# A hybrid encoder layer in float32 on one core: gate and up of 16 of 22 F-tile pairs by seven block products in place of eight

## The chip, the cores and the metric

The kernel runs on one core of a Trainium2 chip. The metric is the time of one execution in microseconds (us) of device time. Five engines take part: TensorE (PE, with its weight loads shown apart as PEld), VectorE (DVE), ScalarE (ACT), GpSimd (POOL) and SyncE (SP), whose queue issues the transfers.

## The reference, cut to what matters

The layer is four sublayers one after the other, each with a norm ahead of it and one behind it: a SwiGLU FFN, a mixer (neighbourhood attention beside a mean pool), a second SwiGLU FFN, and a gated embedding. Tokens are 512, features 1024, and the FFN has 2816 hidden features. Everything is float32.

```
def rms_norm(x, g):
    xf = x.astype(jnp.float32)
    y = xf * lax.rsqrt(jnp.mean(xf * xf, axis=-1, keepdims=True) + RMS_EPS)
    return (y * g.astype(jnp.float32)).astype(x.dtype)

def swiglu(x, w_gate, w_up, w_down):
    return (jax.nn.silu(x @ w_gate) * (x @ w_up)) @ w_down

h = x + 0.5 * rms_norm(swiglu(rms_norm(x, g1pre), ...), g1post)
h = h + rms_norm(hybrid_mixer(rms_norm(h, gmpre), ...), gmpost)
h = h + 0.5 * rms_norm(swiglu(rms_norm(h, g2pre), ...), g2post)
h = h + rms_norm((p @ W_proj) * sigmoid(rms_norm(h, gppre) @ W_gate), gppost)
```

## The kernel before, in words

Everything is kept transposed: features on the 128 partitions, the 512 tokens along the free axis, so the residual h is eight tiles of 128x512. A float32 product is made of three TensorE matmuls on float32r operands: each operand is split into a high part (the value rounded) and a low part (what is left), and `mm3` (lines 227 to 231) multiplies high by high (L228), high weight by low input (L229) and low weight by high input (L230).

**The weight stream.** All weights of the layer are one list of chunks of 128x1024 float32 (512 KB). `Stream.load` (L182) has SP load a chunk into one of NRAW=2 raw tiles; `Stream.pump` splits it, the high part `whi` by a cast on ACT (L195), the low part `wlo` by a subtraction on DVE (recorded as L160, the helper `tt` of all two-input operations). There are NB=8 pairs of split tiles. A chunk holds the stationary tiles of two k tiles times four output tiles.

**The FFN** (`ffn`, L411). The 22 F tiles of gate and up go in 11 groups of two tile pairs. A group (`group`, L344, `emit_group`, L308) makes four output tiles (gate and up of two F tiles) in four PSUM banks from 4 chunks: 8 k tiles x 4 output tiles x 3 matmuls = 96 matmuls of 512 columns. The input of those matmuls is `uh`/`ul`, the split of h times the norm's gain, without the norm's factor of the token. That factor, `rb` (one value per token, on every partition), is multiplied onto gate by DVE (`t<-g,rb`); then ACT makes Silu (L422), DVE multiplies by up (`v<-g,t`), ACT casts to `zh` (L430) and DVE makes `zl`. The factor of the up half is put off to the norm behind the sublayer (`norm` with `scaled`, tile `veps`). After groups 0 to 2, 3 to 6 and 7 to 10 (`PARTS`) come the down products of that part, with `zh`/`zl` as input and `f` as the running sum, each in two halves of the output. The last down group of a sublayer (`last_group`, L369) runs by halves of the tokens, in matmuls of 256 columns, so that the norm and the residual update of the first half (`boundary`, L395) go beside the products of the second.

**What sets the order.** The kernel emits its work with a clock of its own (`Clock`, `Task`, the table `TIMES`), and a scheduler then fixes the order on each engine. Each engine works through its list in order, and so do the queues of SP and POOL. The splits run ahead of the products by as many chunks as there are split tiles. At a sublayer's end `last_group` holds its chunks to the end, and the splits that run ahead meanwhile (`ahead`, L387) are for the first products of the next sublayer; in the mixer the eight bias tiles `bm` are loaded early by 64 small loads on SP into tiles with the tag "y".

Of the kernel before, what the change touches and what calls it, by code (L numbers as in the profile page):

```python
# [27 lines left out]
NB = 8  # L28
NRAW = 2
SPLIT_AHEAD = 4  # L30
# Where steps go between the products: distances on the emission clock, by sublayer boundary, head pair or channel group.
# [14 lines left out]
    "out": 3.8,  # L46
    "held": 2,
# [6 lines left out]
class Task:  # L54
    """Work emitted in steps: a generator that yields how long (us of products) to wait before its next step."""
# [7 lines left out]
class Clock:  # L63
    """Orders the emission: time advances with the products emitted, and due steps of tasks go between them."""
# [50 lines left out]
def kernel(  # L115
# [50 lines left out]
    class Stream:  # L166
        def __init__(self):
            self.loaded = 0
            self.split = 0
            self.done = 0  # L170
            self.hold = False
            self.freed = set()
            self.raw = {}
            self.parts = {}

        def load(self, upto):
            while self.loaded < min(upto, n_chunks):
                c = self.loaded
                self.raw[c] = wraw.tile([P, CH], F32, tag="raw", name=f"raw{c}")
# [3 lines left out]
                self.loaded += 1  # L183

        def pump(self, upto):
            while self.split < min(upto, self.done + NB, n_chunks):
                c = self.split
                self.load(c + 1)
                raw = self.raw.pop(c)
# [3 lines left out]
                for i in range(0, CH, w):  # L193
                    sl = slice(i, i + w)
                    nc.scalar.copy(hi[:, sl], raw[:, sl])  # L195
                    tt(lo[:, sl], raw[:, sl], f32(hi[:, sl]), ALU.subtract)
                self.parts[c] = (hi, lo)
                self.split += 1
                self.load(self.split + NRAW)
# [54 lines left out]
    veps = act.tile([P, NT], F32, name="veps")  # L254
# [17 lines left out]
    def norm(sl, rc, wait, scaled=False):  # L272
# [11 lines left out]
        if scaled:  # L284
            for b in range(nb):
                nc.scalar.activation(sd[:, b:b + 1], ps[:, b:b + 1], AF.Sqrt, bias=veps[:, b0 + b:b0 + b + 1],
                                     scale=1.0 / D)
        else:
            nc.scalar.activation(sd[:, :nb], ps[:, :nb], AF.Sqrt, bias=eps, scale=1.0 / D)
        if rc is not None:  # L290
            nc.vector.tensor_scalar(veps[:, b0:b0 + nb], ps[:, :nb], EPS / D, EPS * EPS, op0=ALU.mult, op1=ALU.add)
# [16 lines left out]
    def emit_group(c0, nch, rhs, ps, sl, free, evac=None, before=None):  # L308
        """All output tiles together, k outermost; with evac, one output tile after the other."""
# [8 lines left out]
        if evac is None:  # L318
            for c in range(nch):
                for kk in range(2):  # L320
                    if before:
                        before(2 * c + kk)
                    for t in range(4):
                        one(c, kk, t)
                if free:
# [11 lines left out]
    def half_banks():  # L337
        """Four accumulators of 256 columns in two banks; the first product of a bank opens both."""
# [5 lines left out]
    def group(c0, nch, rhs, evac, late=()):  # L344
        ps = [bank("g") for _ in range(4)]
        emit_group(c0, nch, rhs, ps, slice(0, S), True)
# [5 lines left out]
    def first_group(c0, rhs, evac, chains):  # L352
        """The first products of a sublayer, by halves of the tokens, as its input comes."""
# [15 lines left out]
    def last_group(c0, nch, rhs, evac, chain):  # L369
        """The last products of a sublayer, by halves of the tokens; returns the tasks that follow each."""  # L370
# [16 lines left out]
    def ahead():  # L387
        """Splits of the chunks that the next sublayer begins with."""
        upto = min(ws.done + NB, n_chunks)
# [5 lines left out]
    def boundary(f, gpost, gnext, scaled):  # L395
        def chain(sl, i):
            yield from norm(sl, None, at("nb", i), scaled)
# [13 lines left out]
    def ffn(chains, gpost, gnext):  # L411
        f = [None] * KD
        late = ()
        for pi, (g0, g1) in enumerate(PARTS):
# [3 lines left out]
            def ev_gu(t, ps, sl, j0, held={}):  # L418
                if t % 2 == 0:
                    g = ttile("t")  # L420
                    tt(g[:, sl], ps, rb[:, sl], ALU.mult)
                    nc.scalar.activation(g[:, sl], g[:, sl], AF.Silu)  # L422
# [3 lines left out]
                if j not in zh:  # L426
                    zh[j], zl[j] = ztile(j)
                v = vtile("v")
                tt(v[:, sl], ps, g[:, sl], ALU.mult)
                nc.scalar.copy(zh[j][:, sl], v[:, sl])  # L430
                tt(zl[j][:, sl], v[:, sl], f32(zh[j][:, sl]), ALU.subtract)

            for gi in range(g0, g1):
                j0 = 2 * (gi - g0)

                def ev(t, ps, sl, j0=j0):
                    ev_gu(t, ps, sl, j0)

                c0 = take(4)
                if gi > 0:  # L440
                    group(c0, 4, u_rhs, ev, late if gi == 1 else ())
                elif len(chains) == 2:
                    late = first_group(c0, u_rhs, ev, chains)
                else:
# [3 lines left out]
                    for t in range(4):  # L448
                        ev(t, ps[t], slice(0, S))

# [10 lines left out]
            for og in range(2):  # L461
# [8 lines left out]
                if lastp and og == 1:  # L470
                    return last_group(take(nch), nch, z_rhs, ev, boundary(f, gpost, gnext, True))
                group(take(nch), nch, z_rhs, ev)

# [1 line left out]
    def mixer(chains, gpost, gnext):  # L475
# [10 lines left out]
        def pieces(t0, t1):  # L486
            """(query order, token order) slices of a [.., 4, 8, 16] view for tokens of tiles t0..t1."""
# [130 lines left out]
        def windows(g, ps):  # L618
            """Centred means of group g minus the tokens themselves, in token order, split."""
# [141 lines left out]
        def m_rhs(k):  # L761
# [4 lines left out]
                          boundary(f, gpost, gnext, False))  # L766

# [91 lines left out]
    chains = ffn([clk.spawn(start(), TIMES["start"])], lambda k: gh[:, k:k + 1], GMPRE)  # L859
    chains = mixer(chains, GMPOST, G2PRE)  # L860
    chains = ffn(chains, lambda k: gh[:, 8 + k:9 + k], GPPRE)
    ple(chains)
    assert cur[0] == n_chunks == ws.done, (cur[0], n_chunks, ws.done)


# [1 line left out]
def _tok(a):  # L867
    """(512, F) with rows in sequence order -> (F, 512), tokens in the order (tile of 16 columns, row, column)."""
# [9 lines left out]
def _stationary(w, cols, nt=4):  # L878
    """Tiles [k][128][cols] -> chunks (2 k tiles each) of [128][k][tile][128]."""
    k = w.shape[0] // P  # L880
    a = np.stack([w[:, c:c + P] for c in cols], 1).reshape(k // 2, 2, P, nt, P)
    return a.transpose(0, 2, 1, 3, 4).reshape(k // 2, P, CH)

# [101 lines left out]
```

## Time and profile before

| what | value |
|---|---|
| three runs | 1114.8, 1114.62, 1113.77 us; median 1114.62 us |
| profiled execution | span 1111.1 us from the first to the last instruction; no time of its own beside the span is given |
| mean granted clock of TensorE | 0.995 of 2.4 GHz |
| PE busy | 1094.0 us (98%), 5610 matmuls |
| DVE busy | 578.6 us (52%) |
| ACT busy | 454.1 us (41%) |
| POOL busy | 0.7 us |
| loaded from and written to memory | 104.93 MB and 2.10 MB, 96 GB/s over the span |

The span leaves out what lies before the first and behind the last instruction, so it stands 3.5 us below the median of the runs. A busy time is the sum of an engine's instruction times, and matmuls overlap: what a stage costs is read from the starts of its instructions. PEclk is the share of its full clock that TensorE was granted.

### The profile page before, as it was taken

The page shows a single profiled execution, that of the slowest core. Times are in us where ns is not written, and L with a number is a line of the kernel's source. Part 1 is how long each engine was busy: PE and PEld are TensorE (multiplying, and loading weights), DVE is VectorE, ACT ScalarE, POOL GpSimd, SP SyncE. Part 2 cuts the span into 40 slices and gives each one's busy share as a digit, 9 for nine tenths or more (in the row PEclk, how much of TensorE's full clock was granted, in tenths as well). Part 3 has the DMA queues.
Part 4 walks back from the last instruction along what each step waited for, and adds up shares of the span by engine and source line. Part 5 has one row for each costly group of instructions (what it writes and reads, how often), then busy time and mean ns, then how long its engine had stood idle before and what let it go on. Part 6 is the DMA issues. An engine that isn't in the chain of part 4 may idle for free.

```text
span 1111.1 us, 14120 instructions
## 1 busy us (share of the span) xinstructions
PE 1094.0 (98%) x5610; PEld 930.1 (84%) x5610; DVE 578.6 (52%) x1041; ACT 454.1 (41%) x765; POOL 0.7 (0%) x6
## 2 busy tenths in 40 slices
PE   9999999999999999999999999999999999999995
PEld 7888888888889988887888899888888888889994
DVE  6642334333434987977444439632334333434976
ACT  7533223212323665366232257523223212323784
POOL 0000000000000000000000000000000000000000
PEclk9999999999999999999999999999999999999998
DMA  6553222232332043231223210533232222332112
GB/s 221 184 162 118 95 95 95 95 94 95 97 97 73 20 133 114 76 95 59 95 95 95 95 58 31 176 117 96 95 95 95 94 95 95 97 99 72 38 58 76
DMA packets 37010, 107.94 MB, mean 97 GB/s; under 512 B 4816, under 2 KB 11472, under 8 KB 36944
## 3 DMA queue, kind: packets, MB, share of 16 engines
q1 hardware_dynamic: 36800, 107.01, 29.8%
q8 instruction: 44, 0.72, 0.3%
q14 instruction: 22, 0.18, 0.1%
q10 hardware_dynamic: 144, 0.03, 0.0%
HBM read 104.93 MB, written 2.10 MB: 96 GB/s over the span
## 4 chain that ended last, share of the span: by engine, by line
PE 94%; DVE 2%; ACT 2%; issue 1%; DMA 0%; SPq 0%; DVEq 0%; ACTq 0%
PE g L228 25%; PE g L230 25%; PE g L229 25%; PE gate L228 2%; PE gate L229 2%; PE gate L230 2%; PE br L228 1%; PE br L230 1%; PE br L229 1%; DVE o L160 1%; ACT e L567 1%; PE v L229 1%; PE xp L228 1%; PE v L228 1%; PE v L230 1%; PE xp L230 1%
## 5 line engine op out<-in xcount | busy, mean ns | idle before, releaser
L160 DVE TENSOR_TENSOR wlo<-raw,whi 128x1024 fp32r<-128x1024 f32 (+1 forms) x195 | 235.3, 1208 | 340.8 <-ACT whi L195 340.2
L195 ACT CAST whi<-raw 128x1024 fp32r<-128x1024 f32 (+1 forms) x195 | 202.1, 1038 | 422.6 <-PE g L229 301.1
L228 PE MATMUL g<-uh,whi 128*128 128x512 f32 (+1 forms) x960 | 345.9, 362 | 0.4 <-ACT whi L195 0.4
L229 PE MATMUL g<-ul,whi 128*128 128x512 f32 (+1 forms) x960 | 346.3, 361 | 0.0
L230 PE MATMUL g<-uh,wlo 128*128 128x512 f32 (+1 forms) x960 | 345.7, 361 | 0.5 <-DVE wlo L160 0.5
L230 PEld LDWEIGHTS g<-uh,wlo 128*128 128x128 f32 x960 | 180.7, 188 | 28.6 <-DVE wlo L160 0.9
L228 PEld LDWEIGHTS g<-uh,whi 128*128 128x128 f32 x960 | 180.7, 188 | 28.3 <-ACT whi L195 0.9
L229 PEld LDWEIGHTS g<-ul,whi 128*128 128x128 f32 x960 | 180.8, 188 | 27.5 <-DVE ul L163 0.2
L228 PE MATMUL g<-zh,whi 128*128 128x512 f32 (+1 forms) x512 | 179.9, 351 | 0.0
L230 PE MATMUL g<-zh,wlo 128*128 128x512 f32 (+1 forms) x512 | 179.0, 350 | 0.0
L229 PE MATMUL g<-zl,whi 128*128 128x512 f32 (+1 forms) x512 | 177.9, 347 | 0.0
L230 PEld LDWEIGHTS g<-zh,wlo 128*128 128x128 f32 x512 | 96.0, 188 | 14.1
L229 PEld LDWEIGHTS g<-zl,whi 128*128 128x128 f32 x512 | 96.1, 188 | 13.6
L228 PEld LDWEIGHTS g<-zh,whi 128*128 128x128 f32 x512 | 96.3, 188 | 12.1
L160 DVE TENSOR_TENSOR acc<-acc,sq 128x256 f32<-128x256 f32 (+1 forms) x96 | 44.7, 466 | 17.9 <-ACT sq L269 16.7
L422 ACT ACTIVATE t<-t 128x512 f32<-128x512 f32 (+1 forms) x46 | 27.9, 610 | 63.5 <-DVE t L160 63.4
L160 DVE TENSOR_TENSOR t<-g,rb 128x512 f32<-128x512 f32 (+1 forms) x46 | 30.5, 667 | 39.6 <-PE g L230 38.4
L228 PE MATMUL gate<-uh,whi 128*128 128x512 f32 x128 | 50.6, 395 | 0.0
L230 PE MATMUL gate<-uh,wlo 128*128 128x512 f32 x128 | 50.0, 390 | 0.0
L229 PE MATMUL gate<-ul,whi 128*128 128x512 f32 x128 | 49.9, 390 | 0.0
L430 ACT CAST zh<-v 128x512 fp32r<-128x512 f32 (+1 forms) x46 | 27.3, 596 | 27.9 <-DVE v L160 27.8
L160 DVE TENSOR_TENSOR zl<-v,zh 128x512 fp32r<-128x512 f32 (+1 forms) x46 | 30.5, 665 | 13.1 <-ACT zh L430 13.1
(150 smaller groups left out, 960.8 us busy)
## 6 DMA issues: line engine op xcount, KB each, us to landing
raw<-in_wst SPq DMA_DIRECT2D x191, 512.0 KB, 3.4
h<-in_x SPq DMA_DIRECT2D x8, 256.0 KB, 5.7
bm<-in_bias SPq DMA_DIRECT2D x64, 32.0 KB, 3.3
out<-o SPq DMA_DIRECT2D x16, 128.0 KB, 1.7
raw<-in_wst SPq DMA_DIRECT2D x4, 128.0 KB, 3.5
g_sb<-in_gains ACTq DMA_DIRECT2D x1, 34.0 KB, 3.0
edge_sb<-in_edge SPq DMA_DIRECT2D x1, 32.0 KB, 5.9
```

The lines of the kernel that those rows point to most:

```text
L160: nc.vector.tensor_tensor(o, a, b, op=op)
L195: nc.scalar.copy(hi[:, sl], raw[:, sl])
L228: nc.tensor.matmul(o, wh, xh, start=first, stop=False, **kw)
L229: nc.tensor.matmul(o, wh, xl, start=False, stop=False, **kw)
L230: nc.tensor.matmul(o, wl, xh, start=False, stop=last, **kw)
L422: nc.scalar.activation(g[:, sl], g[:, sl], AF.Silu)
L430: nc.scalar.copy(zh[j][:, sl], v[:, sl])
L567: nc.scalar.activation(e[:, ii, :], e[:, ii, :], AF.Exp, bias=mn[:, ii:ii + 1], scale=-1.0, accum_out=sm[:, ii:ii + 1])
```

## The change

Groups 3 to 10 of both FFNs (`FAST`), which is 8 of 11 groups each, are computed by `fast_group`. Such a group is a product of a 2x2 block matrix of weights (rows: the two F tiles, gate and up beside each other; inner: the two halves of the 1024 features) by a 2x2 block matrix of inputs (inner halves by the left and the right 256 tokens). Seven block products stand in for eight. Each block product is 2 output tiles (gate, up) x 4 k tiles x 3 = 24 matmuls of 256 columns, 168 in a group.

The rest of the change serves those groups:

- **Sums of weights.** A fast group needs its four weight blocks and four sums of blocks. Two sums (`s3`, `s1`) are made in the load: SP loads one block, and then an accumulating transfer on GpSimd's queue (L210) adds the other onto it. Two are made by DVE on raw tiles (`source`). A fast group so takes five plain loads on SP's queue and two accumulating ones on GpSimd's, seven splits (seven casts on ACT, seven subtractions on DVE) and two additions of 128x1024 on DVE, where a group before took four loads and four splits.
- **Sums of products.** The products gather in three PSUM banks p, q, r. ACT copies three intermediate results away (`kept`: m1, m16, m7), and the next products are added onto the same banks; DVE makes three of the four result blocks (`made`) and the fourth is p itself. Then come Silu and the product with up per block, 128x256 each.
- **Sums of inputs.** `normalized` makes the normed input `un` with the factor rb, `renew` splits it over again into `uh`/`ul` during group 1, and `combined` makes four sums of its blocks and splits them, in tiles with the tags "y", "pth", "ptl" and "e". From group 2 on the input has the factor rb in it, so gate needs no multiplication by rb, and groups 0 and 1 get one more; the norm behind the sublayer has no `scaled` any more.
- **Buffers.** NB falls from 8 to 6 split tiles, NRAW rises from 2 to 6 raw tiles, loaded two ahead.

The core of the diff:

```diff
+FAST = range(3, 11)
-NB = 8
-NRAW = 2
+NB = 6
+NRAW = 6
+RAW_AHEAD = 2
...
+        ITEMS = ((0, 2), (0, 1), (1,), (2,), (3,))
+        LOADS = (4, 5, 5, 5, 5, 5, 5)
...
-                    nc.sync.dma_start(self.raw[c][:, i:i + w], wst[c][:, i:i + w])
+                    nc.sync.dma_start(self.raw[n][:, i:i + w], wst[c][:, i:i + w])
+                for c in more:
+                    nc.gpsimd.dma_start(self.raw[n], wst[c], accum_op=ALU.add)
...
+            if i == 2:
+                tt(a11, a11, s1, ALU.add)
+            if i == 6:
+                tt(a12, a12, a11, ALU.add)
+            return ((a11, ()), (a12, ()), (a11, ()), (s3, (c,)), (s1, (c + 1,)), (a22, (c + 2,)),
+                    (a12, (c + 3, c + 4)))[i]
...
+        def product(i, o, first):
+            wh, wl = ws.get(c0 + i)
+            for t in range(2):
+                for kk in range(4):
+                    w = slice((kk * 2 + t) * P, (kk * 2 + t + 1) * P)
+                    xh, xl = moving(i, kk)
+                    mm3(o[:, t * 256:(t + 1) * 256], wh[:, w], wl[:, w], xh, xl,
+                        first and kk == 0 and t == 0, kk == 3, skip_group_check=True)
+            ws.free(c0 + i)
...
+        product(0, p, True)
+        m1 = kept("m1", p)
+        product(1, q, True)
+        made(0, 0, q, m1, ALU.add)
+        product(2, p, False)
+        m16 = kept("m16", p, acc)
+        product(3, r, True)
+        m7 = kept("m7", r)
+        product(4, p, False)
+        made(1, 1, m7, p, ALU.subtract)
+        product(5, r, False)
+        made(1, 0, r, m16, ALU.subtract)
+        product(6, p, False)
+        done(0, 1, p, True)
...
+        def renew(k):
+            for c in chains:
+                clk.need(c)
+            while k not in un:
+                clk.need(whole, whole.steps + 1)
+            nc.scalar.copy(uh[k], un[k])
+            tt(ul[k], un[k], f32(uh[k]), ALU.subtract)
```

**ACT in a gate and up group.** Before, ACT casts one chunk after another until the next group's Silu (`t<-t`) comes; this is a stretch in the middle part of the first FFN:

```order
L195 CAST whi_1756<-raw_1692 128x1024
L195 CAST whi_1786<-raw_1730 128x1024
L195 CAST whi_1816<-raw_1760 128x1024
L195 CAST whi_1868<-raw_1790 128x1024
L195 CAST whi_1898<-raw_1820 128x1024
L195 CAST whi_1928<-raw_1872 128x1024
L422 ACTIVATE t<-t 128x512
```

In the changed kernel the same engine, at the passage from one fast group to the next (`raw_1568` and `raw_1574` hold the next group's blocks a11 and a12, L473 are the copies m1, m16 and m7, L580 are Silus):

```order
L242 CAST whi_1503<-raw_1323 128x1024
L553 CAST zh<-v 128x512
L242 CAST whi_1537<-raw_1331 128x1024
L473 COPY m_1477<-p 128x512
L242 CAST whi_1570<-raw_1568 128x1024
L580 ACTIVATE w<-w 128x256
L242 CAST whi_1604<-raw_1574 128x1024
L473 COPY acc<-p 128x512
L242 CAST whi_1638<-raw_1568 128x1024
L473 COPY m_1578<-r 128x512
```

The copies of PSUM banks now stand behind casts of chunks that have just been loaded: the copy of m16 (`acc<-p`) comes after the casts of a11 and a12 of the next group.

**The queues of SP and POOL.** SP's loads of one fast group in the changed kernel, in order (a22, a11 and a12 of a group, then the first blocks of the sums s3 and s1 of the next):

```order
L208 DMA raw_1323<-in_wst 128x1024
L208 DMA raw_1325<-in_wst 128x1024
L208 DMA raw_1331<-in_wst 128x1024
L208 DMA raw_1333<-in_wst 128x1024
L208 DMA raw_1436<-in_wst 128x1024
```

and POOL's, where each row is the second block of a sum, added onto the tile that SP loaded:

```order
L210 DMA raw_1090<-in_wst 128x1024
L210 DMA raw_1193<-in_wst 128x1024
L210 DMA raw_1333<-in_wst 128x1024
L210 DMA raw_1436<-in_wst 128x1024
```

Before, POOL's list held no transfer. Now each accumulating one waits for the plain load of the same tile, and the cast of the sum waits for both.

**DVE at the end of the first FFN.** Before, from the last residual tile of the first half of the tokens to the first input tile of the second half:

```order
L163 SCALAR_TENSOR_TENSOR h_87<-t,gh,h_87 128x256
L294 RECIPROCAL rc<-sd 128x2
L160 TENSOR_TENSOR acc<-acc,sq 128x256
L163 SCALAR_TENSOR_TENSOR ul_102<-h_86,g_sb,uh_94 128x256
L163 SCALAR_TENSOR_TENSOR ul_103<-h_87,g_sb,uh_95 128x256
L163 SCALAR_TENSOR_TENSOR dl<-ident,rc,dh 128x128 x2
L160 TENSOR_TENSOR acc<-acc,sq 128x256
L160 TENSOR_TENSOR wlo_3039<-raw_2539,whi_3038 128x1024
L160 TENSOR_TENSOR t<-f_764,rb 128x256
```

and in the changed kernel:

```order
L167 SCALAR_TENSOR_TENSOR h_87<-t,gh,h_87 128x256
L330 RECIPROCAL rc<-sd 128x2
L164 TENSOR_TENSOR wlo_3733<-raw_3303,whi_3732 128x1024
L167 SCALAR_TENSOR_TENSOR ul_102<-h_86,g_sb,uh_94 128x256
L167 SCALAR_TENSOR_TENSOR dl<-ident,rc,dh 128x128 x2
L167 SCALAR_TENSOR_TENSOR ul_103<-h_87,g_sb,uh_95 128x256
L164 TENSOR_TENSOR acc<-acc,sq 128x256
L164 TENSOR_TENSOR wlo_3790<-raw_3362,whi_3789 128x1024
L164 TENSOR_TENSOR t<-f_852,rb 128x256
```

Two splits of weights stand in this stretch instead of one.

## Rows read from the trace of the kernel before

**Rows 1.** The page: span, busy time of each engine, chain that ended last.

```profile
span 1111.1 us, 14120 instructions
...
PE 1094.0 (98%) x5610; PEld 930.1 (84%) x5610; DVE 578.6 (52%) x1041; ACT 454.1 (41%) x765; POOL 0.7 (0%) x6
...
PE 94%; DVE 2%; ACT 2%; issue 1%; DMA 0%; SPq 0%; DVEq 0%; ACTq 0%
```

**Rows 2.** Timeline of PE, groups 3 to 6 of the first FFN: start, duration.

```profile
105.64 0.40 PE L228 MATMUL g<-uh,whi 128*128 128x512 f32 x1
105.87 0.39 PE L229 MATMUL g<-ul,whi 128*128 128x512 f32 x1
...
192.73 0.40 PE L228 MATMUL g<-zh,whi 128*128 128x512 f32 x1
```

**Rows 3.** By stretch: length, busy (count) of PE, PEld, DVE, ACT, POOL, PEclk, DMA, GB/s.

```profile
28.45:72.44 43.99, 43.99 (x197) 36.42 (x196) 24.18 (x27) 20.19 (x24) 0.00 (x0) 1.00 0.59 187
105.64:192.50 86.86, 86.86 (x384) 71.89 (x383) 32.17 (x36) 24.87 (x31) 0.00 (x0) 1.00 0.30 97
```

**Rows 4.** Timeline of PE, last down group of the first FFN: 256 columns, first and last.

```profile
345.77 0.28 PE L228 MATMUL g<-zh,whi 128*128 128x256 f32 x1
345.89 0.28 PE L229 MATMUL g<-zl,whi 128*128 128x256 f32 x1
...
360.14 0.28 PE L230 MATMUL g<-zh,wlo 128*128 128x256 f32 x1
```

**Rows 5.** Timeline of PE, last group of the fourth sublayer: 256 columns of `uh`.

```profile
1071.44 0.28 PE L229 MATMUL g<-ul,whi 128*128 128x256 f32 x1
...
1087.04 0.28 PE L230 MATMUL g<-uh,wlo 128*128 128x256 f32 x1
```

**Rows 6.** Groups of DVE by form: busy, mean ns, idle before and what ended it.

```profile
L160 DVE TENSOR_TENSOR wlo<-raw,whi 128x1024 fp32r<-128x1024 f32 x191 | 233.7, 1224 | 340.7 <-ACT whi L195 340.2
L160 DVE TENSOR_TENSOR acc<-acc,sq 128x256 f32<-128x256 f32 x80 | 33.7, 421 | 13.5 <-ACT sq L269 12.6
L160 DVE TENSOR_TENSOR t<-g,rb 128x512 f32<-128x512 f32 x42 | 28.9, 691 | 39.5 <-PE g L230 38.4 <-ACT rb L305 1.1
L160 DVE TENSOR_TENSOR zl<-v,zh 128x512 fp32r<-128x512 f32 x42 | 28.9, 688 | 13.1 <-ACT zh L430 13.1
L163 DVE SCALAR_TENSOR_TENSOR ul<-h,g_sb,uh 128x512 fp32r<-128x512 f32 x8 | 5.8, 751 | 1.4 <-ACT uh L261 1.4
```

**Rows 7.** Groups of ACT by form.

```profile
L195 ACT CAST whi<-raw 128x1024 fp32r<-128x1024 f32 x191 | 200.5, 1051 | 422.5 <-PE g L229 301.1 <-PE gate L229 42.9 <-PE br L229 28.0
L430 ACT CAST zh<-v 128x512 fp32r<-128x512 f32 x42 | 25.8, 614 | 27.9 <-DVE v L160 27.8
L455 ACT COPY f<-g 128x512 f32<-128x512 f32 x16 | 9.4, 585 | 11.1 <-PE g L230 10.3
L793 ACT ACTIVATE g<-g 128x256 f32<-128x256 f32 x16 | 6.4, 411 | 4.2 <-DVE g L160 4.2
```

**Rows 8.** The page's DMA issues: KB each, median us to landing.

```profile
raw<-in_wst SPq DMA_DIRECT2D x191, 512.0 KB, 3.4
```

**Rows 9.** L182, all weight loads: duration of an issue in ns, and landing.

```profile
L182 SPq DMA_DIRECT2D raw<-in_wst x195: 327/328/432, 1.2 to 1062.9; - x195
...
DMA to landing us min/median/max: 2.8/3.4/6.1
```

**Rows 10.** Timeline of DVE at the end of the first FFN.

```profile
376.83 1.22 DVE L160 TENSOR_TENSOR wlo<-raw,whi 128x1024 fp32r<-128x1024 f32 x1
377.96 0.42 DVE L160 TENSOR_TENSOR t<-f,rb 128x256 f32<-128x256 f32 x1
...
379.70 0.48 DVE L163 SCALAR_TENSOR_TENSOR ul<-h,g_sb,uh 128x256 fp32r<-128x256 f32 x1
...
388.13 0.49 DVE L163 SCALAR_TENSOR_TENSOR ul<-h,g_sb,uh 128x256 fp32r<-128x256 f32 x1
```

**Rows 11.** Timeline of PE there: first uses of those two `ul` tiles.

```profile
381.45 0.28 PE L229 MATMUL g<-ul,whi 128*128 128x256 f32 x1
...
389.30 0.28 PE L229 MATMUL g<-ul,whi 128*128 128x256 f32 x1
```

More of the change, by code (lines that the diff above doesn't have):

```diff
@@ L172, in __init__ @@
             self.freed = set()
+            self.over = set()
             self.raw = {}
@@ L176, in load, with drop, source @@
         def load(self, upto):
-            while self.loaded < min(upto, n_chunks):
-                c = self.loaded
-                self.raw[c] = wraw.tile([P, CH], F32, tag="raw", name=f"raw{c}")
+            while (self.loaded < min(upto, len(self.items))
+                   and (self.loaded < NRAW or self.loaded - NRAW in self.over)):
+                n = self.loaded
+                c, *more = self.items[n]
+                self.raw[n] = wraw.tile([P, CH], F32, tag="raw", name=f"raw{n}")
                 w = CH // 4 if c < 1 else CH
                 for i in range(0, CH, w):
-                    nc.sync.dma_start(self.raw[c][:, i:i + w], wst[c][:, i:i + w])
+                    nc.sync.dma_start(self.raw[n][:, i:i + w], wst[c][:, i:i + w])
+                for c in more:
+                    nc.gpsimd.dma_start(self.raw[n], wst[c], accum_op=ALU.add)
                 self.loaded += 1
+        def drop(self, *items):
+            for n in items:
+                del self.raw[n]
+                self.over.add(n)
+        def source(self, n):
+            kind, c, i = self.ops[n]
+            if not kind:
+                return self.raw[c], (c,)
+            s3, s1, a22, a11, a12 = (self.raw.get(c + j) for j in range(5))
+            if i == 2:
[4 more added lines that the diff above has]
+                    (a12, (c + 3, c + 4)))[i]
         def pump(self, upto):
-            while self.split < min(upto, self.done + NB, n_chunks):
+            while self.split < min(upto, self.done + NB, self.n):
                 c = self.split
-                self.load(c + 1)
-                raw = self.raw.pop(c)
+                self.load(self.needs[c])
+                assert self.loaded >= self.needs[c]
+                raw, over = self.source(c)
                 hi = wsp.tile([P, CH], F32R, tag="whi", name=f"whi{c}")
@@ L196, in pump @@
                     tt(lo[:, sl], raw[:, sl], f32(hi[:, sl]), ALU.subtract)
+                self.drop(*over)
                 self.parts[c] = (hi, lo)
                 self.split += 1
-                self.load(self.split + NRAW)
+                self.load(self.needs[c] + RAW_AHEAD)
         def get(self, c):
@@ L283, in norm @@
         sd = tmp.tile([P, NT], F32, tag="sd", name="sd")
[L284 to L291, printed above, removed]
+        nc.scalar.activation(sd[:, :nb], ps[:, :nb], AF.Sqrt, bias=eps, scale=1.0 / D)
         if rc is None:
@@ L408, in boundary, with fast_group, kept, made @@
         return chain
-    def ffn(chains, gpost, gnext):
+    LEFT, RIGHT = HALVES
+    def fast_group(c0, moving, done):
+        p, q, r = (bank(n) for n in "pqr")
+        def product(i, o, first):
[7 more added lines that the diff above has]
+            ws.free(c0 + i)
+        def kept(name, o, tile=None):
+            k = wide(name, "sq")[:, 0:S] if tile is None else tile
+            nc.scalar.copy(k, o)
+            return k
+        def made(row, column, a, b, op):
+            w = ttile("w")
+            tt(w, a, b, op)
+            done(row, column, w, False)
+        product(0, p, True)
[12 more added lines that the diff above has]
+        done(0, 1, p, True)
@@ L882, in _stationary, with plan, _quad @@
     return a.transpose(0, 2, 1, 3, 4).reshape(k // 2, P, CH)
+def plan():
+    ffn = []
+    for g0, g1 in PARTS:
+        for g in range(g0, g1):
+            ffn += [True] if g in FAST else [False] * 4
+        ffn += [False] * (2 * (g1 - g0))
+    mixer = [False] * (4 * 4 + 1 + 16 + 8 + 8)
+    return ffn + mixer + ffn + [False] * (1 + 2 + 8)
+def _quad(w, pairs):
+    out = []
+    for i, j in ((1, 0), (1, 1), (0, 0), (0, 1)):
+        a = np.stack([w[j * 512:(j + 1) * 512, pair[i]:pair[i] + P] for pair in pairs], 1)
+        out.append(a.reshape(4, P, 2, P).transpose(1, 0, 2, 3).reshape(1, P, CH))
+    return np.concatenate(out, 0)
 def _ffn_chunks(wg, wu, wd):
```

123 lines of the change are left out of this document (99 added, 24 removed).

## The prediction

> **What bounds the kernel now.** I began with the page. Of a span of 1111.1 us PE is busy for 1094.0, and the chain that ended last lies on PE for 94% [rows 1]. DVE and ACT are at 52% and 41%, POOL does nothing. So the time is the row of matmuls, one behind the other, and a change is worth what it takes out of that row, unless another engine makes PE wait.
>
> Next I read what one gate and up group costs. The timeline of PE has the first matmul of group 3 at 105.64 us and the first down matmul behind group 6 at 192.73: 87.09 us for 4 x 96 = 384 matmuls, 0.2268 us each, so 21.77 us per group [rows 2]. In that stretch PE is never idle, the granted clock is 1.00 (2.4 GHz), and DVE is busy for 32.17 of 86.86 us, ACT for 24.87 [rows 3]. There is room on both, and the DMA share is 0.30.
>
> The width that the change uses is in the trace as well. The last down group of the first FFN runs matmuls of 256 columns: 345.77 to 360.14 us, 122 intervals, 14.37 / 122 = 0.1178 us each [rows 4]. With `uh` as input, at the end of the layer, 130 intervals take 1071.44 to 1087.04, 0.1200 each [rows 5]. Each of them has a weight load of its own, as in the change, so the loads are in these numbers.
>
> **The change, part by part.**
>
> **Matmuls.** A fast group has 7 x 24 = 168 matmuls of 256 columns. At 0.119 us, the middle of the two stretches, that is 19.99 us against 21.77: 1.78 less. For 16 groups: **-28.5 us**. With 0.1200 it is 20.16 and -25.8; with 0.1178, 19.79 and -31.7. Seven eighths of 21.77 would be 19.05; the rest goes to the part of a matmul that does not shrink with its columns, 0.119 against half of 0.2268, on 168 matmuls.
>
> The Trainium skill speaks against the change here: "TensorE: Matmul & The Clock Gate", section "Back-to-back issue gap", gives sustained spacings of 131 ns at 512 columns and 81 ns at 128. On a line between them 256 columns would take 98 ns (an estimate), a group would go from 12.6 to 16.5 us, and the kernel would lose about 62 us. The trace doesn't agree: its 512 columns take 226.8 ns and its 256 columns 117.8 to 120.0, and the measurement decides.
>
> **Work on DVE and ACT within a fast group.** DVE has 7 subtractions and 2 additions of 128x1024 (the subtraction starts 1.13 us ahead of the next instruction [rows 10]), 5 two-input operations of 128x512 (0.69) and 4 of 128x256 (0.42) [rows 6]: 10.2 + 3.5 + 1.7 = 15.4 us. ACT has 7 casts of 1.05, 3 copies of a bank (0.585), 2 casts of `zh` (0.614) and 4 Silus of half width (0.411) [rows 7]: 7.4 + 1.8 + 1.2 + 1.6 = 12.0 us. Both are below 20.0, so neither sets the pace by its sum; what is left is when each result is due.
>
> **Loads.** A fast group takes 7 blocks of 512 KB, 3.67 MB in 20.0 us, 183 GB/s. The stretch from 28.45 to 72.44 us moved 187 GB/s at a DMA share of 0.59, and PE was busy for all of it [rows 3]. So the plain traffic fits. No row has an accumulating load. A plain one lands after 3.4 us [rows 8], 2.8 to 6.1 [rows 9]. I bound the accumulating one by 3.4 below and 12.2 above, twice the longest, since it also reads the tile that it writes; I take 5 to 7, twice a quick plain one.
>
> **The copies of the banks.** Here a new wait can arise: products 4, 5 and 6 write onto banks that ACT or DVE must have read, and in ACT's order the copy of m16 stands behind the casts of the next group's a11 and a12, whose raw tiles are loaded late. From the start of product 0, with 2.86 us per product: the split of a22 follows product 6 of the group before, a Silu, a cast and a subtraction, and is done by 2.9 us. That frees the raw tile for the next a11, and SP issues a11 and a12 at 2.9 and 3.3 (an issue takes 0.33 [rows 9]). Alone, a11 lands at 6.3; beside the accumulating load of s1 and the other loads I put 6.4 to 7.4 for it and 8.0 to 9.4 for a12 (3.3 + 6.1). Then come the cast of a11, a Silu, the cast of a12 (1.05) and the copy (0.59): done between 9.7 and 11.1. Product 4 writes p at 4 x 2.86 = 11.4. That is in time by 0.3 to 1.7 us. The copy of m7 is due at 14.3 and could be done by 12.2, the block w from m7 and p at 17.2 and done by 15.1. Twelve of the 16 groups are followed by another fast group and have this step. Since the margin at its narrow end is smaller than the spread of landings, I take 0.2 us per group, 12 x 0.2 = **+2.4 us**, bounds 0 and 18 (1.5 us each, the first rival).
>
> **Boundaries.** With 6 split tiles for 8, two splits of the next sublayer's weights now stand in DVE's chain behind `last_group` where one stood. That is 1.13 us more [rows 10] on a chain that PE waits for soon: the `ul` tile done at 380.18 is used at 381.45, the one done at 388.62 at 389.30 [rows 10, 11], margins of 1.27 and 0.68. So between 0 and 1.13 us at each of three boundaries, about 1.13 - 0.68 where the margin is narrow, less where work behind it makes up: **+1.0**, bounds 0 and 3.4.
>
> **Sums of the inputs, the mixer and the start.** Per FFN DVE makes 8 tiles `un`, 8 new `ul`, 16 half-wide sums and 8 low parts: 8 x 0.75 + 16 x 0.69 + 16 x 0.42, some 24 us [rows 6]. They are due before group 3, and up to that lie groups 1 and 2 and two down groups, 44 us with 24.2 us of DVE's work [rows 3] and 2 x 72 x 0.2268 = 33 us with 6 splits. They are hidden by that; if a tile were late, groups 2 or 3 would wait for it by one operation, 0.7 us. The copies of the bias tiles, no longer free to start early, move behind the fast groups on SP's queue, ahead of weights that are due 20 us later. Two split tiles less in the mixer leave less cover for a late load; a few small operations of the norm go. Together **+0.5**, bounds -1 and +3.
>
> **Sum.** -28.5 + 2.4 + 1.0 + 0.5 = -24.6. The span of 1111.1 becomes 1086.5; the runs' median, 1114.62, stands 3.5 above that span, and I keep this: **1090.0 us**.
>
> **The rivals.**
>
> *The loads of a11 and a12 come late.* The accumulating loads take DMA time on the same 16 engines, a12 lands after 11 us instead of by 9.4, the copy of m16 is done at 12.9, and product 4 waits for 1.5 us. For it: the margin is thin, and ACT works in order, so that a load holds up a copy that has nothing to do with it. Against: the traffic fits by the rate shown. 1090.0 - 2.4 + 12 x 1.5 = **1106**. Chance 0.14.
>
> *The accumulating loads can't keep up (the other side).* Two of them per group stand on one queue, one behind the other. If one takes A us, a group can't be shorter than 2A. It decides from 2A = 20.0, and outweighs the gain from 20.0 + 27.0 / 12 = 22.3, A = 11.1 us. At the upper bound of 12.2 a group takes 24.4: 1087.6 + 12 x 4.4 = **1140**. A mechanism that would do this: GpSimd gets at its transfers only while DVE is free, (20.0 - 15.4) / 20.0 = 0.23 of the time, and 3.4 / 0.23 is 14.8. For it: nothing in the trace prices such a load. Against: it needs more than three times a plain load. Chance 0.09, of it 0.07 slower, 0.02 about as before.
>
> Beside this rival stands the Trainium skill, "SBUF — State Buffer", section "SBUF: two separate sides": while VectorE runs an operation in a mode that takes both ports, GpSimd can't write the descriptors of its own transfers, and the DMA engines wait. No run before the change shows it, since POOL's list held no transfer.
>
> *The narrow matmuls don't stay at 0.119.* Fast groups break even at 21.77 / 168 = 0.1296 us. The end of a group, with its change of bank and of weights every 24 matmuls, could cost that. For it: the rate was read in stretches of one kind of input. Against: the stretches with `zh` and with `uh` differ by 0.002. At 0.1296 the time is 1114.6 + 3.9 = **1118.5**. Chance 0.03, of it 0.02 slower and 0.01 same.
>
> That the change doesn't do what it says (some groups still of eight products) I give 0.01, counted as slower.
>
> **How the numbers follow.** The forecast has 0.73: from 1083 (all matmul terms at 0.1178, no waits) to about 1098. With the first rival it is 0.87, and the range **1083 to 1108** ends just behind that rival; with the tails of both it holds about 8 in 10. A measurement of this kernel tells about 0.2%, 2.2 us, from no change. Faster by more: 0.73 + 0.14 = **0.87**; the same: 0.02 + 0.01 = **0.03**; slower: 0.07 + 0.02 + 0.01 = **0.10**.
>
> **What would show it.** PE's timeline: 168 starts of 256 columns in 20.0 us per fast group at 0.119. The waits of PE: a line for `p` released by ACT's copy, up to 3 us in all if I am right, 18 if the loads are late; then ACT's cast waits for the DMA of raw. The transfers of L210: landing by 7 us if right, above 11 if they can't keep up, with DVE's or ACT's waits for the sum behind them. PE idle at the three boundaries below 3.4 us in all. I am wrong if fast groups take over 21 us, if the starts lie at other than 0.118 to 0.120, or if the time goes to the stretch ahead of group 3.

## The result, and the profile after

The changed kernel takes **1094.95 us** (median of 4 runs, 1093.82 to 1095.48) against 1114.3 of the kernel before: a ratio of 0.9828, 95% interval 0.9814 to 0.9842, 19.4 us less. Forecast were 1090.0 and 1083 to 1108.

The page of the changed kernel, the lines that answer to [rows 1]:

```profile
span 1093.7 us, 17000 instructions
PE 1073.1 (98%) x6762; PEld 963.1 (88%) x6762; DVE 729.2 (67%) x1247; ACT 542.1 (50%) x921; POOL 28.8 (3%) x38
PE 93%; ACT 3%; DVE 3%; issue 1%; DMA 0%; DVEq 0%; ACTq 0%
```

PE still bounds it. The spans differ by 17.4 us and the medians by 19.4. A run of the changed kernel lies 1.8 us above its span, and so do the runs of the kernel before that were made beside the experiments. So the 3.5 us that the prediction put around the span of before were too many: with 1.8, the profiled execution of before took 1112.9, less than each of its runs, while that of the changed kernel, 1095.48, is the longest of its four. Stages are compared by the two spans.

PE's timeline of the changed kernel, the beginning of group 3, of the down products behind group 6, and of group 7:

```profile
109.70 0.29 PE L276 MATMUL p<-uh,whi 128*128 128x256 f32 x1
...
189.65 0.40 PE L276 MATMUL g<-zh,whi 128*128 128x512 f32 x1
189.88 0.40 PE L277 MATMUL g<-zl,whi 128*128 128x512 f32 x1
190.12 0.39 PE L278 MATMUL g<-zh,wlo 128*128 128x512 f32 x1
...
234.45 0.28 PE L276 MATMUL p<-uh,whi 128*128 128x256 f32 x1
```

Four fast groups take 109.70 to 189.65, 79.95 us for 672 matmuls: 0.1190 each, 19.99 us per group. The 87.09 us of [rows 2] have become 79.95, four times over: -28.6 us. The rest gives 11 us back, in three places:

| stage | before, us | after, us | difference |
|---|---|---|---|
| start to the first down product of FFN 1 | 72.66 | 76.10 | +3.4 |
| fast groups, 4 stretches of four | 348.4 | 319.8 | -28.6 |
| the 864 down matmuls of 512 columns in the FFNs and 96 at the mixer's end | 219.8 | 224.0 | +4.2 |
| all else (mixer, boundaries, end) | | | +3.5 |

The down products are the surprise. In the rows above they start 0.23 to 0.24 us apart; the 192 from 189.65 to 234.45 take 0.2333 each. In the kernel before, the same 192 run from 192.73 [rows 2] to the first matmul of group 7, 0.2290 each:

```profile
236.69 0.40 PE L228 MATMUL g<-uh,whi 128*128 128x512 f32 x1
```

The row "all else" splits into 1.5 us from the last down group of FFN 1 to the mixer's last products, 0.9 from there to the first down product of FFN 2, and 1.2 behind that FFN's down products. Of the 1.5, 0.7 have the same look as the down products: the mixer's 192 branch products (`br`), whose inputs oh, ol, yh and yl were moved by the change as well, go from 0.2296 to 0.2333 us.

PE's waits in the changed kernel (total us, times, longest):

```profile
PE nb L339 <- ACT dh L335: 3.9, 2, 2.2
PE nsum L324 <- DVE acc L164: 3.5, 3, 2.5
PE warm L1004 <- DVE ones L999: 1.1, 1, 1.1
PE g L278 <- DVE wlo L164: 0.9, 1, 0.9
```

No line has p, q or r: no fast group makes PE wait. (The four lines left out are below 1 us each and wait for tiles of other stages.) Of the waits for nb, 1.7 us are new and lie behind 30 us, in the first FFN's norm:

```profile
32.16 0.39 PE L339 MATMUL nb<-dh,ones_r 128*128 128x256 f32 x1 [1.70 <-ACT dh L335]
```

The rest of the 3.4 us at the start is of another kind: in this execution the first ten matmuls start some 0.43 us apart instead of 0.227, 2.0 us in all. The view has a clock of 1.00 for that stretch:

```profile
5.00:9.40 4.40, 4.35 (x10) 3.47 (x11) 3.01 (x7) 3.26 (x7) 0.00 (x0) 1.00 1.02 336
```

That 1.00 measures nothing: the trace's records of the granted clock begin at 9.71 us, with 1.00 (2.4 GHz), and where there is no record the view counts no loss. The 0.43 us are what matmuls of 512 columns take in a stretch recorded at 1.2 GHz (experiment 4), so this looks like the lower level of the clock, though no record covers it. In the twelve profiled executions the records begin between 4.1 and 10.1 us, and the slow matmuls end there: 4.62 for the kernel before, which has none, 8.96 for pad224 below, which has eight, 5.12 for x128. Of the eleven executions of other programs than before, five begin with eight to ten such matmuls and six with none to four; pad224 and x128, whose programs begin alike, are on either side, so this part is not put down to the change. One stretch of four fast groups, columns as in [rows 3]:

```profile
109.70:189.64 79.94, 79.94 (x673) 79.94 (x672) 58.61 (x67) 43.50 (x64) 4.36 (x5) 1.00 0.60 166
```

DVE is busy for 14.7 us per group (15.4 were worked out), ACT for 10.9 (12.0), the DMA share is 0.60. The accumulating transfers, by the page's DMA issues and by their line:

```profile
raw<-in_wst SPq DMA_DIRECT2D x207, 512.0 KB, 3.7
raw<-in_wst POOLq DMA_DIRECT2D x32, 512.0 KB, 5.7
```

```profile
L210 POOL DMA_DIRECT2D raw<-in_wst x32: 865/871/1013, 66.1 to 929.8; - x32
...
DMA to landing us min/median/max: 5.4/5.7/9.1
```

An accumulating load lands after 5.7 us in the median, within the 5 to 7 that were assumed, and even the longest, 9.1, is below the 11.1 at which two of them outlast a group.

### The profile page after: what moved, and what is told of

Read it like the earlier page. It is cut to its first block, busy times and chain, and to the rows that moved or that the text cites. A ratio compares the mean times of both kernels' runs of the same rounds, so it can differ in the third digit from the quotient of the medians.

```text
span 1093.7 us, 17000 instructions
## 1 busy us (share of the span) xinstructions
PE 1073.1 (98%) x6762; PEld 963.1 (88%) x6762; DVE 729.2 (67%) x1247; ACT 542.1 (50%) x921; POOL 28.8 (3%) x38
## 4 chain that ended last, share of the span: by engine, by line
PE 93%; ACT 3%; DVE 3%; issue 1%; DMA 0%; DVEq 0%; ACTq 0%
PE g L276 15%; PE g L278 15%; PE g L277 15%; PE p L277 6%; PE p L276 6%; PE p L278 6%; PE r L277 3%; PE r L278 3%; PE r L276 3%; PE gate L276 2%; PE gate L277 2%; PE gate L278 2%; PE q L278 1%; PE q L277 1%; PE q L276 1%; PE br L276 1%
## 5 line engine op out<-in xcount | busy, mean ns | idle before, releaser
L277 PE MATMUL g<-ul,whi 128*128 128x256 f32 (+1 forms) x448 | 147.8, 331 | 0.2 <-DVE ul L167 0.2
L278 PE MATMUL g<-uh,wlo 128*128 128x256 f32 (+1 forms) x448 | 146.9, 331 | 0.9 <-DVE wlo L164 0.9
L276 PE MATMUL g<-uh,whi 128*128 128x256 f32 (+1 forms) x448 | 146.8, 332 | 0.6 <-ACT whi L242 0.6
L278 PEld LDWEIGHTS g<-zh,wlo 128*128 128x128 f32 x512 | 96.1, 188 | 14.7
L278 PEld LDWEIGHTS g<-uh,wlo 128*128 128x128 f32 x448 | 85.3, 191 | 8.8 <-DVE wlo L164 1.0
L277 PEld LDWEIGHTS g<-ul,whi 128*128 128x128 f32 x448 | 85.6, 191 | 8.3 <-DVE ul L167 0.6
L276 PEld LDWEIGHTS g<-uh,whi 128*128 128x128 f32 x448 | 85.2, 191 | 8.5 <-ACT whi L242 0.9
L277 PE MATMUL p<-ul,whi 128*128 128x256 f32 x256 | 72.4, 283 | 0.0
L278 PE MATMUL p<-uh,wlo 128*128 128x256 f32 x256 | 72.4, 283 | 0.0
L276 PE MATMUL p<-uh,whi 128*128 128x256 f32 x256 | 72.4, 283 | 0.0
L277 PE MATMUL p<-x,whi 128*128 128x256 f32 x256 | 72.0, 281 | 0.0
L276 PE MATMUL p<-x,whi 128*128 128x256 f32 x256 | 71.6, 280 | 0.0
```

What stands on the lines that cost most here:

```text
L276: nc.tensor.matmul(o, wh, xh, start=first, stop=False, **kw)
L277: nc.tensor.matmul(o, wh, xl, start=False, stop=False, **kw)
L278: nc.tensor.matmul(o, wl, xh, start=False, stop=last, **kw)
```

## The experiments

**1. The place of the moving tiles.** The change dropped the tile `veps`, 16 bytes that took up 32. By the programs' tables of addresses every tile behind it moved down by 32 bytes in each partition: zh and zl stood 64 above a multiple of 256 before the change, and stand 32 above one after it; uh and ul stand at a multiple of 256 in both. (The traces hold no addresses; the steps between the runs below are in their edits.) Is that why the down matmuls are slower? An empty tile puts them elsewhere (what follows a # in the cuts of code is added here):

```diff
     rb = act.tile([P, S], F32, name="rb")
+    pad = act.tile([P, 8], F32, name="pad")     # pad32; 56 for pad224, 24 for pad96
     rc_pre = act.tile([P, NT], F32, name="rc_pre")
```

> The changed kernel with an empty tile of 32 bytes per partition ahead of rc_pre, which moves every tile behind it by 32 bytes: zh, zl, oh, ol, yh, yl and the sums x again stand at a multiple of 64 bytes, 64 above a multiple of 256, as zh stood before the change; uh and ul stay at a multiple of 256. Theory (the place of the moving tile sets the spacing of its matmuls): the down matmuls of 512 columns go from 0.2333 back to 0.229 us, some 1090 of them, -4.7; those of 256 columns go from 0.1167 to 0.1178, +0.6; the products with x in the fast groups go from 0.118 by as much, +1.7; together about 1092.5 us against 1094.95. Rival (the spacing of the down matmuls rose since more transfers and more work of DVE run beside them): 0.2333 stays, and the time too, 1095.

> The same with an empty tile of 224 bytes: zh, zl and the sums x stand at a multiple of 256 bytes, as uh does. Theory (place of the moving tile): they take the spacings that uh shows, 0.2268 at 512 columns (about -7 us in all) and 0.1200 at 256 columns (+1.9 for zh, +2.7 for the products with x, a fast group 20.16 us); together about 1092.5 us. Rival (traffic beside them): spacings and time stay, 1095.

> The same with an empty tile of 96 bytes: zh and x stand at a multiple of 128 that is none of 256. If only the place within 128 bytes counts, spacings as with the 224 bytes: 0.2268 and 0.1200. If the place within 256 counts, other values, between 0.2268 and 0.2333. Rival (traffic): 0.2333 as now.

| kernel | zh above a multiple of 256 | 512 columns of zh, us | four fast groups, us | time, us |
|---|---|---|---|---|
| changed | 32 | 0.2333 | 79.95 | 1094.95 |
| pad32 | 64 | 0.2290 in the first part and at the mixer's end, 0.2333 in the other parts | 79.92 to 80.09 | 1093.56 |
| pad224 | 0 | 0.2268 | 80.26 | **1090.21** |
| pad96 | 128 | 0.2324 to 0.2333 | 79.23 to 79.42 | 1093.44 (one run) |

The timeline of the kernel pad224, down products behind group 6 and the start of group 7:

```profile
188.63 0.40 PE L276 MATMUL g<-zh,whi 128*128 128x512 f32 x1
188.86 0.40 PE L277 MATMUL g<-zl,whi 128*128 128x512 f32 x1
...
232.18 0.28 PE L276 MATMUL p<-uh,whi 128*128 128x256 f32 x1
```

43.55 us for 192, 0.2268 each, as uh has it. The same work lies beside them as in the changed kernel, so traffic alone is not the cause; the address is. Nor is it the weights' address: the products with uh, which no pad moves, use the same split tiles and keep 0.2267 to 0.2269 at 512 columns (in pad96 in FFN 2; its FFN 1 has a stretch at half the clock) and 0.1192 to 0.1201 in the first two products of a fast group in all four kernels. The ratio of pad224 to the kernel before is 0.979 (0.9777 to 0.9804), clear of the changed kernel's 0.9828 (0.9814 to 0.9842); that of pad32, 0.9821 (0.9807 to 0.9834), is not. pad32 was only half foretold: zh stood where it had stood before, and 0.2290 came back in the first part of each FFN and at the mixer's end, but in the other parts 0.2333 stayed. So the distance to a multiple of 256 doesn't say all; what else counts there, another tile's place or the accumulating loads beside these parts, was not tried. A second thing stands in the table: the fast groups go the other way, slowest with the multiple of 256 (80.26) and quickest with 128 above one (79.23).

**2. Each matmul at its better place.** The sums x go 128 above a multiple of 256 (those in the tag y), zh and zl to a multiple of 256:

```diff
+    pad = act.tile([P, 56], F32, name="pad")
+    def place(name, pool):
+        if name not in pads:
+            pads[name] = pool.tile([P, 32], F32, tag=name, name=name, bufs=1)
...
     def ztile(j):
+        if j >= 4:
+            place("padz", act)
...
             if n < 4:
+                place("padx", act)
                 return [act.tile([P, S], F32R, tag="y", name="x", bufs=8) for _ in range(2)]
+            place("padt", tmp)
             if n < 6:
```

> The changed kernel with the empty tile of 224 bytes, and two more of 128 bytes that put the sums x 128 above a multiple of 256 (those in the tag y) while zh and zl stay at a multiple of 256. Theory (place of the moving tile): the down matmuls at 0.2268 as with 224 bytes, the fast groups at 79.2 us for four as with 96 bytes, instead of 80.3; the branch products with yh lose some 0.8 us; about 1087. Rival (what was gained in the run with 96 bytes came from something else): 1090.2, as with 224 bytes.

**1086.4 us**, ratio 0.9761 (0.9748 to 0.9775). Both terms are there: down products at 0.2268, four fast groups in 79.25. But the second lies mostly elsewhere than in the tag y. Against pad224, the two products with the x of the tag y go from 0.1200 us per matmul to 0.1188, the two with the x of the tags pth, ptl and e from 0.1179 to 0.1141 and 0.1147: some 0.7 of the 1.0 us per four groups. Where those tiles stand is not on record. And for the tag y 128 above a multiple of 256 is not the best place: in the changed kernel these two products take 0.1166.

**3. The start, and the buffers.** First the kernel before with the changed numbers of tiles alone, which leaves all other places as they were:

```diff
-NB = 8
-NRAW = 2
+NB = 6
+NRAW = 6      # before_nb6; NRAW = 2 in before_nb6raw2
```

> The kernel before with 6 split tiles for 8 and 6 raw tiles for 2, and nothing else; all other tiles keep their places. Theory (fewer split tiles cost time where casts wait for a free tile and hold up the norm behind them on ACT, at the start and at the boundaries): 3 to 4 us slower, about 1118, with a wait of PE for nb of 1.5 to 2 us near 30 us, as in the changed kernel. Rival (that wait comes from the new work on the inputs): no change, 1114.3, and no such wait.

> The kernel before with 6 split tiles for 8, and 2 raw tiles as it had. In the run with 6 of each, two more splits stood ahead of the last sum of squares on DVE at the start, since with 6 raw tiles their chunks are there earlier. Theory A (the 6 raw tiles cost: chunks that come early have their splits put ahead of the norm): with 2 raw tiles most of the 10.5 us go, within 2 us of 1113.9. Theory B (the 6 split tiles cost: casts wait for a free tile): it stays near 1124.

With 6 and 6 it takes **1124.47 us** against 1113.91, ratio 1.0098 (1.0084 to 1.0112), with 6 and 2 **1117.25** against 1113.38, ratio 1.0035 (1.0021 to 1.0049). So neither theory had it all: two split tiles less cost 3.9 us, six raw tiles some 7 more on this kernel. (It asks for chunks as far ahead as it has raw tiles, the changed one two ahead, so the 7 are not the changed kernel's.) By the traces, the 6 split tiles alone cost 0.8 us at the start, 1.8 between the mixer's last products and the first down product of FFN 2, and 1.5 behind its down products; with 6 raw tiles these are 3.2, 5.9 and 1.5, and 1.5 in the mixer. The 5.9 hold a wait of PE for a sum of squares (`nsum`), 2.92 us up to 702.76, and a stretch at half the clock (0.50, 1.2 GHz) behind it:

```profile
699.60:702.70 3.10, 0.24 (x3) 0.04 (x1) 2.65 (x7) 3.09 (x8) 0.00 (x0) 0.89 0.69 223
703.60:708.80 5.20, 5.20 (x13) 4.11 (x14) 3.74 (x7) 1.41 (x4) 0.00 (x0) 0.50 0.61 188
```

The rival of the first run, that the new work on the inputs makes the wait for nb, falls: the wait is there without that work (29.96 us, 1.97 between two starts). It is gone with 2 raw tiles.

How raw tiles can cost time is in DVE's timeline. The changed kernel at the start:

```profile
18.26 1.48 DVE L164 TENSOR_TENSOR acc<-acc,sq 128x512 f32<-128x512 f32 x2
19.66 3.49 DVE L164 TENSOR_TENSOR wlo<-raw,whi 128x1024 fp32r<-128x1024 f32 x3
23.07 0.68 DVE L164 TENSOR_TENSOR acc<-acc,sq 128x512 f32<-128x512 f32 x1
23.68 2.35 DVE L164 TENSOR_TENSOR wlo<-raw,whi 128x1024 fp32r<-128x1024 f32 x2
25.95 0.15 DVE L330 RECIPROCAL rc_pre<-sd 128x2 f32<-128x2 f32 x1
```

Three splits stand ahead of the last sum of squares, and two more ahead of the reciprocal that the norm needs. In the kernel before, one split stands ahead of that sum and none ahead of the reciprocal:

```profile
19.21 1.22 DVE L160 TENSOR_TENSOR wlo<-raw,whi 128x1024 fp32r<-128x1024 f32 x1
20.35 0.69 DVE L160 TENSOR_TENSOR acc<-acc,sq 128x512 f32<-128x512 f32 x1
...
22.42 0.15 DVE L294 RECIPROCAL rc_pre<-sd 128x2 f32<-128x2 f32 x1
```

With free raw tiles the chunks come earlier, and the scheduler puts their splits first. The next run holds the early loads back and leaves the tiles as they are:

```diff
                 w = CH // 4 if c < 1 else CH
+                if 2 <= n < 10:
+                    nc.vector.tensor_copy(self.raw[n][:, 0:1], f32(self.last[:, 0:1]))
                 for i in range(0, CH, w):
...
                 self.parts[c] = (hi, lo)
+                self.last = lo
```

> The changed kernel, where each of the chunks 2 to 9 is loaded only when the chunk two ahead of it is split, as 2 raw tiles would have it (a copy of one column from that chunk's low part into the raw tile, ahead of the load). Theory A: the start takes 3.4 us less, group 3 begins near 106.3 us for 109.7, the wait of PE for nb of 2 us is gone; about 1092. Theory B (6 split tiles): no gain, 1095, or a loss from the eight small copies.

DVE's timeline at the start of that kernel:

```profile
18.92 1.21 DVE L164 TENSOR_TENSOR wlo<-raw,whi 128x1024 fp32r<-128x1024 f32 x1
20.05 0.68 DVE L164 TENSOR_TENSOR acc<-acc,sq 128x512 f32<-128x512 f32 x1
20.65 0.14 DVE L208 COPY raw<-wlo 128x1 f32<-128x1 f32 x1
20.84 0.69 DVE L164 TENSOR_TENSOR acc<-acc,sq 128x512 f32<-128x512 f32 x1
23.51 0.17 DVE L333 RECIPROCAL rc_pre<-sd 128x2 f32<-128x2 f32 x1 [1.98 <-ACT sd L330]
```

The reciprocal comes 2.4 us earlier, the wait at 30 us is gone, and group 3 begins at 107.54 for 109.70. The time is 1093.34 us, ratio 0.9819 (0.9805 to 0.9832); against the changed kernel the intervals overlap, so the 2.2 us are shown by the trace more than by the times. The same for every plain chunk (condition `n in self.plain and n - 2 in self.plain`):

> The same for every plain chunk with a plain chunk two ahead of it, so also in the mixer, the down groups and the boundaries. Theory A: the boundaries lose their extra waits as well (1.0 at the mixer's end, 1.2 ahead of the embedding, part of 0.9 at the first FFN's end), another 2 to 3 us, about 1089.5. Theory B: the boundaries stay, or are slower, since with 6 split tiles and later loads there is less cover: 1092 to 1097.

1094.8 us, ratio 0.9836 (0.9823 to 0.985): no gain. One wait at a boundary shrinks (a product ahead of the embedding waits for a split, 1.18 between two starts at 1032.45 us of the changed kernel; at that place 0.66 is left), others come (for nsum, 1.17 at 672.32). The wait ahead of the embedding is in before_nb6raw2 as well, with 1.17 at 1054.17, and not in the kernel before: it is the price of 6 split tiles, and 2 raw tiles don't undo it.

**4. Both together.** The edits of x128 and gate_start:

> Both at once: the places of the run x128 and the held loads at the start of the run gate_start. If the two terms are independent (spacings by place, order of the splits at the start), they add: 1086.4 less about 2 us, and another 1 to 2 us since no wait of 2 us stands ahead of group 1 any more, about 1083.5. If they are not, 1086.4.

**1084.2 us**, ratio 0.9739 (0.9726 to 0.9753): the terms add as far as the intervals tell (the two ratios taken together would give 0.9752), 29 us below the kernel before and the fastest of all runs here. The first down product begins at 73.06 us where the run x128 had 77.48. The profiled execution of x128 had lost more than the wait, as its stretches show:

```profile
30.00:32.40 2.40, 0.71 (x4) 0.42 (x3) 1.32 (x2) 1.91 (x4) 0.00 (x0) 1.00 0.94 372
32.40:35.70 3.30, 3.30 (x10) 2.60 (x9) 1.56 (x4) 0.37 (x1) 0.00 (x0) 0.50 0.60 180
```

PE waits for nb up to 31.97 us, and in the stretch from 32.4 the granted clock is 0.50 (1.2 GHz): the matmuls start 0.43 us apart for 0.2268.

**5. How much room the accumulating loads have.** Each is issued twice:

```diff
-                for c in more:
+                for c in more * 2:
```

> The changed kernel with each accumulating transfer issued twice, so that the two sums of weights take their second block twice (the sums are other numbers, the work behind them is the same). It measures how much room those transfers have. A single one lands in 5.7 us. If they have the room worked out ahead (the sum s1 is due some 11.5 us behind its plain load), two take 11.4 and PE waits for nothing or below 1 us per group: 1095 to 1107. If they were near the limit already, as the rivals had it, 2 to 5 us per group with a fast group behind it: 1119 to 1155, slower than the kernel before.

**1129.44 us**, ratio 1.0136 (1.0116 to 1.0156), slower than the kernel before: the rivals' box. PE's waits in that kernel, and one of them on DVE, ACT and PE:

```profile
PE r L276 <- ACT m L473: 20.1, 8, 4.3
```

```profile
141.60 1.23 DVE L164 TENSOR_TENSOR raw<-raw,raw 128x1024 f32<-128x1024 f32 x1 [3.52 <-DMA raw<-in_wst]
```

```profile
142.92 1.04 ACT L242 CAST whi<-raw 128x1024 fp32r<-128x1024 f32 x1 [4.55 <-DVE raw L164]
143.87 0.58 ACT L473 COPY m<-r 128x512 f32<-128x512 f32 x1
```

```profile
144.50 0.39 PE L276 MATMUL r<-x,whi 128*128 128x256 f32 x1 [1.99 <-ACT m L473]
```

Read upwards: PE waits for a copy of its bank that has nothing to do with the late load. The copy stands behind a cast on ACT, the cast waits for a DVE addition, and the addition for the sum s1. In the eight groups with such a wait the two transfers of s1 take 11.9 to 15.2 us from the first issue to the last landing, since the first lands after 7 to 9 us in six of them, in four beside the second of s3. That is past the 11.5 us of room. One transfer has less left than its 5.7 us suggest: in the changed kernel that of s1 takes 5.5 to 9.1, in ten of the 16 groups the addition starts 0.1 to 4.6 us behind its landing (in the others 9 to 13), and once DVE waits 1.0 us for it. The waits of PE here come to 21.9 us, and behind five of the eight the granted clock falls:

```profile
295.00:299.00 4.00, 0.58 (x5) 0.38 (x4) 2.82 (x3) 1.54 (x3) 0.00 (x0) 0.83 0.00 0
299.00:304.00 5.00, 4.95 (x23) 4.96 (x24) 3.97 (x5) 1.36 (x2) 0.00 (x0) 0.50 0.39 108
```

93 matmuls of the fast groups start some 0.21 us apart instead of 0.119, 9 us more.

## Why the prediction was right, and where it was off

- **Matmuls, -28.5.** -28.6 measured, 0.1190 per matmul. The two stretches of 256 columns [rows 4, 5] priced it: the products with uh take 0.1197 to 0.1201, those with x 0.1166 (tag y) and 0.1198 to 0.1200 (the others), 0.1183 in the mean. That the middle was right is part luck, since the place of x decides: 79.23 to 80.26 for four groups in the runs of experiment 1.
- **The copies of the banks, +2.4.** Nothing. In all 16 groups the copy of m16 ended 10.25 to 10.30 us into the group, and product 4 began at 11.44. The hand-made schedule had 9.7 to 11.1. But the reason for that place was wrong: ACT's rows show what the cast ahead of the copy waited for (group 4, which begins at 129.69; below them the first matmul of product 4).

```profile
138.41 1.06 ACT L242 CAST whi<-raw 128x1024 fp32r<-128x1024 f32 x1 [1.51 <-PE p L277]
139.37 0.58 ACT L473 COPY acc<-p 128x512 f32<-128x512 f32 x1
```

```profile
141.13 0.28 PE L276 MATMUL p<-x,whi 128*128 128x256 f32 x1
```

  It waited for PE, that is for a split tile that product 2 frees, not for the load. With 6 split tiles a cast can't come earlier than a product's end, so the load of a12 had more time than was counted, and the margin is the same 1.14 to 1.19 us in every group.
- **Loads and queues.** The traffic fits, as the stretch at 187 GB/s had it [rows 3]. GpSimd was not kept from its transfers by a busy DVE: in the stretch of four fast groups DVE was busy for 73%, and the transfers of the kernel landed after 5.7 us in the median. The Trainium skill's trap of "SBUF — State Buffer", section "SBUF: two separate sides", is tied to a mode that takes both ports; these rows show no trace of it. Whether an operation here ran in that mode, no row tells. The rival on the late loads fails since in that stretch no cast of ACT waits for a load by the trace, the one on the accumulating loads at 5.7 us per transfer. Experiment 5 shows that the second one's end is real, and PE's waits come there by another chain than the one given: s1, the addition, a cast and the copy of m7. It also makes four transfers per group of two, so how much of the delay of s1 is their number on the queue is not parted.
- **Boundaries, +1.0, and sums of the inputs, mixer and start, +0.5.** Together +1.5 forecast with a bound of +6.4; measured +3.4 at the start, 2.0 of it in slow first matmuls that come and go, and +2.8 elsewhere without the branch products, 6.2. This is the term that was mis-sized. At the three boundaries PE idles 2.1 us for 0.2 before, 1.9 more, which is within the bounds given. The start was taken as hidden, with the price put on the new work of the inputs; experiment 3 puts its wait on the raw tiles, which let splits stand ahead of the norm, and shows that two split tiles less cost 3.9 us on the kernel before. The prediction had looked at DVE's order at the boundary and not at the start.
- **What was not in the sum.** The down products, +4.2 us, and the branch products, +0.7, by their new places. A step of the change that computes nothing, dropping `veps`, moved every tile behind it. With the 32 bytes given back (pad32) the branch products and 384 of the 960 down products have their old spacing, 2.4 us in all; for the other 576, 2.5 us, pad224 shows that the place counts, and what keeps them at 0.2333 in pad32 stays open.
- **The balance.** -28.6 + 6.2 + 4.9 = -17.5 by the spans, against -24.6; the medians have -19.4.

## What to carry to other kernels

Where a resource is widened (raw tiles here) to feed one stage, look at what it lets move ahead in every other stage: an order made by a scheduler fills the room with work that is early, ahead of work that is due. When an allocation is added or dropped, compare the spacing of matmuls that the edit doesn't touch; if it changed, look at the addresses of their moving tiles (the tiles that are streamed past the weights, here uh, zh and x). A wait on an engine that works in order is priced by what stands behind it: a late sum of weights stops a copy of a bank, and a wait of PE of some us can cost clock behind it as well.

## What the runs showed of the hardware

- The spacing of matmuls depends on the address of the moving tile within the partition. At a multiple of 256 bytes it was 0.2268 us for 512 columns and 0.1198 to 0.1200 for 256; 32 above one 0.2333 and 0.1167; 64 above one 0.2290 to 0.2333 and 0.1178; 128 above one 0.2324 to 0.2333 and 0.1187 (all with the zh of the FFNs). Long and short matmuls so prefer different places. The shortest spacing of 256 columns, 0.1141, was that of x in tiles whose place is not on record. Why, and what else counts, was not settled.
- A transfer of 512 KB that adds onto its tile landed after 5.7 us in the median (5.4 to 9.1), a plain one after 3.7 in the same kernel; where two were put on the same tile, one behind the other, the median was 5.8 each (5.3 to 10.0).
- Behind some waits of PE the granted clock was 0.50 (1.2 GHz), and matmuls started 0.43 (512 columns) and 0.21 us (256) apart: five of the eight of experiment 5 (1.85 to 4.30 us), 2.92 us in before_nb6, 1.69 in x128. Others left no such stretch: 1.70 us at 32.16 of the changed kernel, 1.99 at 144.50 in experiment 5.
